# Chunked attention of the last block: keys and values held in rings of six blocks, queries in three buffers, bias in two

## The chip, the core and the metric

The kernel runs on one core of one Trainium2 chip. The metric is the device time of one execution in microseconds (us). A core has five engines with queues of their own: TensorE (PE, matrix products; its weight loads are shown apart as PEld), VectorE (DVE), ScalarE (ACT), GpSimd (POOL) and SyncE (SP), which here issues nearly all DMAs. Each engine works through its own instructions in order and waits on semaphores for the others. TensorE's clock has two levels, 2.4 and 1.2 GHz; the profile gives the granted share of the higher one.

## The reference

Two transformer blocks follow each other on 2048 tokens of width 1024. The change lies in the second one, in its chunked attention with a relative bias, for 8 heads of 64 values:

```
def chunked_relpos_attention(q, k, v, rel_bias):      # CHUNK = 64, N_LEFT_CHUNKS = 8, BAND = 576
    ...
    def one_chunk(c):
        start = c * CHUNK
        qc = lax.dynamic_slice_in_dim(q, start, CHUNK, axis=1)
        kc = lax.dynamic_slice_in_dim(k_pad, start, BAND, axis=1)
        vc = lax.dynamic_slice_in_dim(v_pad, start, BAND, axis=1)
        s = jnp.einsum('bqhd,bkhd->bhqk', qc, kc).astype(jnp.float32) * scale + bias[None]
        ...
        p = jax.nn.softmax(s, axis=-1).astype(v.dtype)
        return jnp.einsum('bhqk,bkhd->bqhd', p, vc)
```

So 64 queries attend to their own 64 keys and the 512 before them. The result is multiplied by silu of a gate. The same block has a second branch with sparse attention (256 chosen keys per query), gates for both branches and an output projection.

## The kernel before

The class `S3` computes the second block. Its projections write what they make into DRAM tensors: `QA` and `KA` (queries and keys of the chunked attention, transposed, each as a rounded part and the rest), `VA` (values, both parts), `QB` and `IQ` for the sparse branch, `SG` and `TZ` for gates. The attention loads from these.

The second block goes in stages (`run`, line 2784). After a first stage of normalization and projections there is `chunked(0)`, chunked attention for the first 1024 tokens; `sparse(range(10))`, sparse attention for ten blocks of 128 queries; `chunked(1)`, chunked attention for the other 1024 tokens; and a tail with the remaining sparse blocks and the output. Beside the first two runs a chain of work called `fill`: the projections of the first 1024 tokens that are still missing (`proj(0, range(8, 32))`), the load of the activations of the next tokens (`xn_load`, tiles `xnh` and `xnl`), and a part of the projections of those. What is left of `fill` runs alone before the next stage. Beside `chunked(1)` runs the rest of the projections, after `keep` has stored three tiles.

The order of instructions is made by the kernel's own planner. Every piece of work is a generator, a lane; `B.run` (line 306) asks the lanes in a fixed order, spawned pieces first, then the front lanes, then `back` (the fill), and begins again at the first as soon as one has issued something. A lane issues an instruction when `B.on` (line 245) says that by the planner's clock (`Clock.op`) its engine and its operands are ready. That clock holds a price for each instruction; for a DMA it is

```
        if eng == "sync":
            self.t[eng] = t + 0.05
            d = self.t["dma"] = max(self.t["dma"], t + 1.1) + cost
            end = d + 0.95
```

with cost = bytes / 3.6e5 us. The order so made is fixed in the program; on the chip the semaphores decide when each instruction starts.

Chunked attention goes by pairs of heads p = 0 to 3, and in each pair by units of 256 queries, c = 4·half to 4·half + 3. `a_loads` (line 2174) loads for each unit: at the first unit of a pair the bias `rb` (one buffer), then `K` of up to 768 keys (two DMAs, one per part, each on 64 partitions), `Q` (four DMAs), and `V` (one DMA); K, V and Q have two buffers each. With c = 0 there are 256 keys, with c = 1 there are 512, else 768. `a_unit` (line 2205) handles 128 queries (t = 0 or 1): score matmuls for both heads and both parts of Q, in pieces of at most 320 columns, under the lock `la`; DVE adds the bias and takes the maximum; ACT makes the exponentials, GpSimd scales them by the reciprocal sum. Then, under the lock `lb`, groups of two tiles are transposed (`pT`), split into two parts by ACT and DVE (`pp`) and multiplied with V (`a_pv`, line 2321). At the end of t = 1 the buffers of K, V and Q are free. ACT and DVE add up the parts (`up`), GpSimd finishes (`ot`), the gate is loaded (`gate_load`, line 2333; for the pair's gate `SG` must have been written by a projection of `fill`), GpSimd multiplies by it and SP stores to `YT`. Four units of 128 queries may be under way at a time (`pipe(self.a_units(half), 4)`, line 2883 on).

Of the kernel before, what the change touches and what calls it, by code (L numbers as in the profile page):

```python
# [22 lines left out]
T = 2048  # L23
# [11 lines left out]
class Clock:  # L35
# [45 lines left out]
    def at(self, a):  # L81
        n = a.tensor.name
        return max(self.ready.get(n, 0.0), self.free.get(n, 0.0))


def is_ap(x):
# [1754 lines left out]
BIG = -(2.0 ** 100)  # L1841
NSTEP = 12
SPLIT = 10


class S3:


    def __init__(self, b, X2, out, comb=None, skip=()):
        self.comb = comb  # L1850
        self.b, self.nc, self.I, self.X2, self.out = b, b.nc, b.I, X2, out
        nc = b.nc
# [276 lines left out]
    def ev_t(self, j, c, ps):  # L2129
        b, nc = self.b, self.nc  # L2130
        s = slice(c * 512, c * 512 + 512)
        if j < 8:
            p, isq = divmod(j, 2)
            sc = 0.125 if isq else 1.0
            hi, lo = yield from self.stage([128, 512], F32R, n=2)
            yield from b.on("scalar", ps, hi)
            nc.scalar.activation(hi, ps, AF.Copy, scale=sc)
            yield 1
            yield from b.on("vector", hi, lo)
            if isq:  # L2140
# [4 lines left out]
            dst = self.QA if isq else self.KA  # L2145
            yield 1
            yield from self.store(dst[0, p, :, s], hi)
            yield from self.store(dst[1, p, :, s], lo, None, ("qa" if isq else "ka", p, c))
        elif j < 16:
            i = (j - 4) % 8  # L2150
            t = yield from self.stage([128, 512])
            yield from b.on("scalar", ps, t)
            nc.scalar.activation(t, ps, AF.Tanh, scale=0.5)
            yield 1
            yield from b.on("vector", t)
            nc.vector.scalar_tensor_tensor(t, t, 1.0, ps, op0=OP.add, op1=OP.mult)
            b.done(ps)
            yield 1
            yield from self.store(self.SG[i, :, s], t, None, ("sg", i, c))
        else:  # L2160
# [10 lines left out]
            yield BLOCK  # L2171


    def a_loads(self, half):

        b, nc, P = self.b, self.nc, self.P
        for p in range(4):
            for c in range(4 * half, 4 * half + 4):
                yield from self.wait(("ka", p, c // 2), ("qa", p, c // 2), *[("va", c * 2 + i, p // 2) for i in range(2)])
                if c % 4 == 0:  # L2180
                    rb = yield from P.get([128, 2, 640], F32, "rb", bufs=self.nrb)
                    yield from b.on("sync", rb)
                    nc.sync.dma_start(rb, self.I["relb"][2 * p:2 * p + 2].rearrange("h q k -> q h k"))
                    yield 1
# [4 lines left out]
                k0 = c * 256 - 512  # L2189
                o = max(0, -k0)  # L2190
                for x in range(2):
                    r = slice(64 * x, 64 * x + 64)
                    nc.sync.dma_start(K[r, :, o:].bitcast(F32), self.KA[x, p, :, k0 + o:k0 + 768].rearrange("(e d) n -> d e n", e=2))
                    for y in range(2):
                        nc.sync.dma_start(Q[r, :, y].bitcast(F32), self.QA[y, p, :, c * 256:c * 256 + 256].rearrange("(e d) n -> d e n", e=2))
                yield 1
                nc.sync.dma_start(V[:, o // 128:].bitcast(F32), self.VA[k0 + o:k0 + 768, p * 256:p * 256 + 256].rearrange("(b t) n -> t b n", t=128))
                if c % 4 == 0:
                    yield from b.on("gpsimd", rb)
                    nc.gpsimd.memset(rb[0:64, :, 576:640], NEG)  # L2200
                    nc.gpsimd.memset(rb[64:128, :, 0:64], NEG)
                self.kv[p, c] = (Q, K, V, rb)
                yield 1

    def a_unit(self, p, c, t):
        b, nc, P = self.b, self.nc, self.P
# [1 line left out]
        while (p, c) not in self.kv:  # L2208
            yield BLOCK
        yield from self.la.get()  # L2210
        Q, K, V, rb = self.kv[p, c]
        k0 = max(0, 512 - blk * 128)
        kts = range(k0 // 128, 5)
        q_ = slice(t * 128, t * 128 + 128)
        sc = []
        st = b.small([128, 8], "ast", bufs=8)
        edges = [k0, 320, 640] if k0 < 320 else [k0, 640]
        for e in range(2):
            s = yield from P.get([128, 640], F32, "sc", bufs=4 if self.stored else 5)
            sc.append(s)  # L2220
            cur, turn = None, [0]
            for x in range(len(edges) - 1):
                w0, w1 = edges[x], edges[x + 1]
                ps = yield from b.bank("pS")
                kk = slice(t * 128 + w0, t * 128 + w1)
                yield from b.on("tensor", Q, K, ps)
                nc.tensor.matmul(ps[:, :w1 - w0], Q[:, e, 0, q_], K[:, e, kk], start=True, stop=False)
                nc.tensor.matmul(ps[:, :w1 - w0], Q[:, e, 1, q_], K[:, e, kk], start=False, stop=True)
# [14 lines left out]
        for g0 in range(0, len(groups), 2):  # L2243
# [8 lines left out]
            yield 1  # L2252
            pend.append((gs, pp, w))
            if len(pend) > 1:
                yield from self.a_pv(po4, V, t, *pend.pop(0), kts, po)
        b.done(*sc)
        while pend:
            yield from self.a_pv(po4, V, t, *pend.pop(0), kts, po)
        self.lb.free()
        if t == 1:  # L2260
            b.done(K, V, Q)
# [56 lines left out]
        w[0] = 1  # L2318
        yield 1

    def a_pv(self, po4, V, t, gs, pp, w, kts, po):
        b, nc = self.b, self.nc
        while not w[0]:
            yield BLOCK
        yield from b.on("tensor", pp, po, V)
        for i, (kt, e) in enumerate(gs):

            nc.tensor.matmul(po4[:, e].rearrange("p x q -> p (x q)"), V[:, t + kt, e * 128:e * 128 + 128], pp[:, i].rearrange("p x q -> p (x q)"),
                             start=kt == kts[0] and e == 0, stop=kt == kts[-1] and e == 1)
        b.done(pp)  # L2330
        yield 1
# [551 lines left out]
    def chunked(self, half, fill, sel):  # L2883

        with self.b.pool("s_a") as P:
            self.P, self.nrb, self.nsel, self.nrl, self.npp = P, 1, 1, 1 if sel else 2, 2 if half and sel else 3
            self.NM = (max(sel, default=0) + 1) * 128
            self.stored.update(sel)
            self.la, self.lb = Lock(1), Lock(1)
            self.kv = {}  # L2890
# [147 lines left out]
```

## Time and profile before

| | |
|---|---|
| median of three runs | 4234.5 us (4229.81 to 4241.1) |
| the profiled execution | 4238.96 us |
| its span, first to last instruction | 4237.1 us |
| mean granted TensorE clock | 0.939 |
| busy: DVE, ACT, POOL | 2733.3, 2263.5, 787.0 us |
| moved by DMA | 815.32 MB, 192 GB/s |
| HBM read, written | 589.56 MB, 229.65 MB |

The profile shows one execution. Rows of instructions name the tile that is written, then those that are read (`pS<-K,Q`); an engine's waits are put down to what ended them. Nearly all instructions have line 111 of the kernel, the helper that records them, so one goes by tiles. Of a window, the row shows each engine's busy time and number of instructions, then the mean granted clock, the mean busy share of the 16 DMA engines, and the rate. Busy times of TensorE are modelled at their ends.

### The profile page before, as it was taken

To read this page: it belongs to the slowest core of one execution; us is meant where nothing else is said; L and a number is where in the kernel's file an instruction comes from. 1 tells how busy PE (TensorE), PEld (TensorE's weight loads), DVE (VectorE), ACT (ScalarE), POOL (GpSimd) and SP (SyncE) were. 2 spreads that over 40 slices of the span, in tenths; PEclk is the share of its full clock that TensorE was granted. 3 is DMA by queue.
4 is the path that set the end of the run, shared out by engine and by line. 5 is a ranking of instruction groups with operands and counts; after the bars stand their busy time and mean duration, and the time that the engine had idled before them with its cause. 6 is when DMAs were issued, how large, how long until landed. Compare 5 with 4: busy or idle time off the path is not lost. (4 is left out here: it accounts for less than half of the span.)

```text
span 4237.1 us, 64813 instructions
## 1 busy us (share of the span) xinstructions
PE 3719.6 (88%) x21649; PEld 3211.7 (76%) x21649; DVE 2733.3 (65%) x7027; ACT 2263.5 (53%) x4628; POOL 787.0 (19%) x1474
## 2 busy tenths in 40 slices
PE   3999999979889995779888899998788979998895
PEld 2888788768768884778777798886677868997685
DVE  7866875787777776562445256777544248878772
ACT  3644645556456664342334167886444238876851
POOL 1310000131011112650334242000222101111000
PEclk9999999979999997899989989999899999999898
DMA  6232542144288886588888834432666488886154
GB/s 221 80 130 73 183 141 90 34 144 140 105 303 316 310 312 248 196 314 275 272 240 265 293 111 133 142 111 63 177 176 189 135 270 299 298 282 222 48 183 172
DMA packets 451953, 815.32 MB, mean 192 GB/s; under 512 B 129712, under 2 KB 269968, under 8 KB 450704
## 3 DMA queue, kind: packets, MB, share of 16 engines
q1 hardware_dynamic: 440080, 777.42, 55.2%
q0 software_dynamic: 11520, 33.57, 2.5%
q8 instruction: 176, 2.88, 0.3%
q14 instruction: 177, 1.45, 0.1%
HBM read 589.56 MB, written 229.65 MB: 193 GB/s over the span
## 5 line engine op out<-in xcount | busy, mean ns | idle before, releaser
L111 PE MATMUL pA<-xnl,whi 128*128 128x512 f32 x1024 | 417.8, 408 | 2.9 <-POOL whi L111 2.9
L111 DVE TENSOR_TENSOR wlo<-ld,whi 128x1024 fp32r<-128x1024 f32 x271 | 325.1, 1230 | 140.4 <-POOL whi L111 74.0
L111 ACT ACTIVATE pp<-pT 128x256 fp32r<-128x256 f32 (+1 forms) x568 | 260.8, 478 | 283.7 <-PE pT L111 277.4
L111 PE MATMUL pA<-xnh,wlo 128*128 128x512 f32 x1024 | 407.1, 398 | 2.3 <-DVE wlo L111 2.3
L111 PE MATMUL pA<-xnh,whi 128*128 128x512 f32 x1024 | 407.5, 398 | 0.0
L111 DVE TENSOR_TENSOR pp<-pT,pp 128x256 fp32r<-128x256 f32 (+1 forms) x568 | 295.9, 539 | 138.7 <-ACT pp L111 135.6
L111 PE MATMUL pA<-hlo,whi 128*128 128x512 f32 x832 | 352.8, 424 | 10.0 <-issue 6.6
L111 PE MATMUL pA<-hhi,wlo 128*128 128x512 f32 x832 | 329.7, 396 | 0.0
L111 PE MATMUL pA<-hhi,whi 128*128 128x512 f32 x832 | 328.9, 395 | 0.0
L111 PE MATMUL pU<-pp,vbS 128*128 128x256 f32 x1088 | 217.2, 311 | 34.5 <-DVE pp L111 23.3
L111 ACT ACTIVATE whi<-ld 128x1024 fp32r<-128x1024 f32 x212 | 213.3, 1052 | 50.7 <-PE pA L111 35.0
L111 DVE SCALAR_TENSOR_TENSOR acc<-rl,iw,acc 128x512 f32<-128x512 f32 (+3 forms) x304 | 212.7, 700 | 36.2 <-ACT rl L111 26.4
L111 PEld LDWEIGHTS pA<-xnh,wlo 128*128 128x128 f32 x1024 | 196.3, 192 | 47.3 <-DVE wlo L111 3.4
L111 PE MATMUL pA<-wlo,xnh 128*128 128x256 f32 (+1 forms) x672 | 205.0, 305 | 24.4 <-ACT st L111 5.9
L111 ACT ACTIVATE bias<-acc,sst 128x384 f32<-128x384 f32 (+13 forms) x168 | 219.9, 1309 | 8.6 <-DVE sst L111 6.1
L111 PEld LDWEIGHTS pA<-xnl,whi 128*128 128x128 f32 x1024 | 197.3, 193 | 33.6 <-POOL whi L111 3.3
L111 PEld LDWEIGHTS pA<-xnh,whi 128*128 128x128 f32 x1024 | 197.3, 193 | 30.2
L111 PEld LDWEIGHTS pU<-pp,vbS 128*128 128x128 f32 x1088 | 164.0, 198 | 53.6 <-DVE pp L111 33.5
L111 PE MATMUL pA<-whi,xnl 128*128 128x256 f32 (+1 forms) x672 | 200.0, 298 | 4.1 <-DMA xnl<-XND 4.1
L111 PE MATMUL pA<-whi,xnh 128*128 128x256 f32 (+1 forms) x672 | 199.8, 297 | 0.0
L111 PE MATMUL pS<-kbS,qd 128*128 128x512 f32 (+3 forms) x640 | 186.4, 391 | 13.5 <-DVE bst L111 9.6
L111 PE MATMUL pS<-K,Q 128*128 128x320 f32 (+3 forms) x480 | 117.7, 354 | 79.8 <-DMA Q<-QA 75.7
(491 smaller groups left out, 10993.7 us busy)
## 6 DMA issues: line engine op xcount, KB each, us to landing
whi<-W2P SPq DMA_DIRECT2D x172, 512.0 KB
wlo<-W2P SPq DMA_DIRECT2D x172, 512.0 KB
ld<-in_w_gu_dram SPq DMA_DIRECT2D x128, 512.0 KB
ld<-in_w_dn_dram SPq DMA_DIRECT2D x64, 512.0 KB
W2P<-whi SPq DMA_DIRECT2D x57, 512.0 KB
W2P<-wlo SPq DMA_DIRECT2D x57, 512.0 KB
Y<-ym SPq DMA_DIRECT2D x48, 512.0 KB
K<-KA SPq DMA_DIRECT2D x48, 384.0 KB
```

Of the source, the lines that this page charges most:

```text
L111: r = real(*a, **k)
```

## The change

Keys and values get one ring each, `K` and `V`, with places for KR = 6 blocks of 256 keys, for a whole stage. A lane of its own, `k_lane`, loads each block once per pair of heads and stage (two DMAs for K, one for V) as soon as the place is free; `pass_blocks` says after each unit which blocks no later unit of the pair needs. `Mark` is a stand-in by which the planner's clock knows when a block has landed; these DMAs are issued past the planner's recording and entered as one operation. `a_loads` loads only Q, with three buffers and two DMAs, from a `QA` whose layout is changed so that both parts of Q lie together. The bias has a lane of its own, `rb_lane`, and two buffers. In `a_unit` the score pieces are cut where the ring ends (`cut`), else at 320 as before. In `go` the lanes stand in the order units, `k_lane`, `a_loads`, `rb_lane`.

```
+KR = 6
-        self.QA = dr("QA", (2, 4, 128, T))
+        self.QA = dr("QA", (4, 4, 64, T))
...
+            dst = [self.QA[p, 2 * y:2 * y + 2, :, s].rearrange("e d n -> (e d) n") if isq else self.KA[y, p, :, s] for y in range(2)]
...
+    def rb_lane(self, half):
+        b, nc, P = self.b, self.nc, self.P
+        for p in range(4):
+            rb = yield from P.get([128, 2, 640], F32, "rb", bufs=self.nrb)
+            yield from b.on("sync", rb)
+            nc.sync.dma_start(rb, self.I["relb"][2 * p:2 * p + 2].rearrange("h q k -> q h k"))
...
+    def k_lane(self, half):
+        b, nc, P, c = self.b, self.nc, self.P, self.b.clock
+        self.K = P.tile([128, 2, 256 * KR], F32R, name="K", bufs=1)
+        self.V = P.tile([128, 2 * KR, 256], F32R, name="V", bufs=1)
+        n = 0
+        for p in range(4):
+            for j in range(max(0, 4 * half - 2), 4 * half + 4):
+                yield from self.wait(("ka", p, j // 2), *[("va", j * 2 + i, p // 2) for i in range(2)])
+                while n - KR >= self.passed:
+                    yield BLOCK
+                m = Mark(f"kv{half}_{n}")
+                c.free[m.tensor.name] = self.freed.get(n - KR, 0.0)
+                yield from b.on("sync", m)
+                o, s = n % KR, slice(j * 256, j * 256 + 256)
+                raw = nc._nc.sync
+                for x in range(2):
+                    raw.dma_start(self.K[64 * x:64 * x + 64, :, o * 256:o * 256 + 256].bitcast(F32),
+                                  self.KA[x, p, :, s].rearrange("(e d) n -> d e n", e=2))
+                raw.dma_start(self.V[:, 2 * o:2 * o + 2].bitcast(F32), self.VA[s, p * 256:p * 256 + 256].rearrange("(b t) n -> t b n", t=128))
+                c.op("sync", [m], [], 2 * 128 * 256 * 4 * 2 / 3.6e5)
...
     def a_loads(self, half):
...
-                K = yield from P.get([128, 2, 768], F32R, "K", bufs=2)
-                V = yield from P.get([128, 6, 256], F32R, "V", bufs=2)
-                Q = yield from P.get([128, 2, 2, 256], F32R, "Q", bufs=2)
-                yield from b.on("sync", K, V, Q)
...
+                Q = yield from P.get([128, 2, 2, 256], F32R, "Q", bufs=3)
+                yield from b.on("sync", Q)
                 for x in range(2):
...
+                    nc.sync.dma_start(Q[64 * x:64 * x + 64].rearrange("d y e n -> d (y e) n").bitcast(F32),
+                                      self.QA[p, :, :, c * 256:c * 256 + 256].rearrange("a d n -> d a n"))
                 yield 1
...
+                js = range(max(0, c - 2), c + 1)
+                while p not in self.rb or any((p, j) not in self.at_ring for j in js):
+                    yield BLOCK
...
+    def pass_blocks(self, p, c, half):
+        last = c if c == 4 * half + 3 else c - 2
+        t = max(self.b.clock.last.get(x.tensor.name, 0.0) for x in (self.K, self.V))
+        for j in range(max(0, 4 * half - 2), last + 1):
+            n = self.last_of[p, j]
+            if n >= self.passed:
+                self.freed[n] = t
+                self.passed = n + 1
...
-        edges = [k0, 320, 640] if k0 < 320 else [k0, 640]
+        cut = k0 + end - r0 if r0 + 640 - k0 > end else 320
+        edges = [k0, cut, 640] if k0 < cut else [k0, 640]
...
-            self.P, self.nrb, self.nsel, self.nrl, self.npp = P, 1, 1, 1 if sel else 2, 2 if half and sel else 3
+            self.P, self.nrb, self.nsel, self.nrl, self.npp = P, 1 if sel else 2, 1, 1 if sel else 2, 2 if half and sel else 3
...
-            self.go(pipe(self.a_units(half), 4), self.a_loads(half), self.sel_lane(sel), back=(fill,))
+            self.go(pipe(self.a_units(half), 4), self.k_lane(half), self.a_loads(half), self.rb_lane(half), self.sel_lane(sel), back=(fill,))
```

In both calls of `chunked`, `sel` is empty.

## Rows read from the trace of the kernel before

**Rows 1.** The page, busy us of each engine (share of the span) and its instructions.
```profile
PE 3719.6 (88%) x21649; PEld 3211.7 (76%) x21649; DVE 2733.3 (65%) x7027; ACT 2263.5 (53%) x4628; POOL 787.0 (19%) x1474
```

**Rows 2.** Windows: stretch and length, busy us (instructions), granted clock, DMA share, GB/s.
```profile
core 0: us, PE busy (x) PEld busy (x) DVE busy (x) ACT busy (x) POOL busy (x), PEclk, DMA share, GB/s
2003.00:2353.00 350.00, 310.24 (x1574) 260.85 (x1573) 177.13 (x549) 127.62 (x315) 136.58 (x195) 0.94 0.86 259
2353.00:2410.00 57.00, 57.00 (x255) 47.23 (x255) 9.26 (x8) 8.19 (x12) 9.42 (x14) 1.00 0.79 276
2410.00:2470.00 60.00, 46.74 (x250) 44.45 (x248) 13.13 (x48) 12.76 (x51) 18.98 (x100) 0.63 0.58 215
2470.00:2890.00 420.00, 406.58 (x2611) 361.25 (x2612) 298.06 (x847) 340.60 (x830) 72.63 (x253) 1.00 0.42 128
2890.00:3003.00 113.00, 79.68 (x434) 60.99 (x432) 72.94 (x213) 61.96 (x114) 6.51 (x19) 0.85 0.22 64
3003.00:3335.00 332.00, 291.52 (x1543) 251.98 (x1543) 162.41 (x571) 142.90 (x343) 94.25 (x163) 0.91 0.66 181
```

**Rows 3.** Waits of PE, 2003 to 2353: total us, times, longest.
```profile
PE pS L111 <- DMA Q<-QA: 26.6, 17, 5.6
PE pU L111 <- DVE pp L111: 4.8, 2, 3.0
...
PE pS L111 <- DMA K<-KA: 1.4, 1, 1.4
```

**Rows 4.** Waits of PE, 3003 to 3335.
```profile
PE pS L111 <- DMA Q<-QA: 36.7, 19, 5.7
PE pS L111 <- DMA K<-KA: 1.6, 1, 1.6
PE pT L111 <- POOL sc L111: 1.4, 2, 1.1
```

**Rows 5.** Timeline: start, duration, engine, operation [idle before it and what ended it].
```profile
2237.32 0.58 SPq L111 DMA_DIRECT2D K<-KA  x1
...
2237.95 1.25 SPq L111 DMA_DIRECT2D Q<-QA  x2
...
2239.24 0.60 SPq L111 DMA_DIRECT2D K<-KA  x1
...
2239.89 1.26 SPq L111 DMA_DIRECT2D Q<-QA  x2
...
2241.24 0.54 SPq L111 DMA_DIRECT2D V<-VA  x1
...
2247.57 1.70 PE L111 MATMUL pS<-K,Q 128*128 128x320 f32 x4 [4.03 <-DMA Q<-QA]
```

**Rows 6.** DMA issues of the whole kernel: count, KB each.
```profile
K<-KA SPq DMA_DIRECT2D x48, 384.0 KB
V<-VA SPq DMA_DIRECT2D x24, 768.0 KB
...
Q<-QA SPq DMA_DIRECT2D x128, 128.0 KB
...
rb<-in_relb_dram SPq DMA_DIRECT2D x8, 640.0 KB
```

**Rows 7.** Waits of PE, 2410 to 2470.
```profile
PE pA L111 <- DMA xnh<-XND: 5.6, 1, 5.6
PE pA L111 <- DMA xnl<-XND: 4.1, 1, 4.1
```

**Rows 8.** Waits of PE, 2890 to 3003.
```profile
PE pS L111 <- DMA Q<-QA: 12.3, 1, 12.3
```

**Rows 9.** Waits of SP's queue, 3003 to 3335.
```profile
SPq L111 <- POOL ot L111: 99.8, 22, 10.7
```

**Rows 10.** Waits of POOL, 3003 to 3335.
```profile
POOL ot L111 <- DMA sg<-SG: 82.5, 16, 9.7
```

**Rows 11.** Waits of POOL, 2003 to 2353.
```profile
POOL ot L111 <- DMA sg<-SG: 29.9, 9, 7.1
```

**Rows 12.** Timeline of SP, 2069 to 2072: the stage's first gate load.
```profile
2070.36 0.80 SPq L111 DMA_DIRECT2D sg<-SG  x2
```

More of the change, by code (lines that the diff above doesn't have):

```diff
@@ L83, in at, with __init__ @@
         return max(self.ready.get(n, 0.0), self.free.get(n, 0.0))
+class Mark:
+    class Named:
+        def __init__(self, name):
+            self.name = name
+    def __init__(self, name):
+        self.tensor = Mark.Named(name)
 def is_ap(x):
@@ L2171, in wait @@
             yield BLOCK
+    def rb_lane(self, half):
[4 more added lines that the diff above has]
+            nc.sync.dma_start(rb, self.I["relb"][2 * p:2 * p + 2].rearrange("h q k -> q h k"))
+            yield 1
+            yield from b.on("gpsimd", rb)
+            nc.gpsimd.memset(rb[0:64, :, 576:640], NEG)
+            nc.gpsimd.memset(rb[64:128, :, 0:64], NEG)
+            self.rb[p] = rb
+            yield 1
+    def k_lane(self, half):
[18 more added lines that the diff above has]
+                c.op("sync", [m], [], 2 * 128 * 256 * 4 * 2 / 3.6e5)
+                self.at_ring[p, j] = (o, m)
+                self.last_of[p, j] = n
+                n += 1
+                yield 1
     def a_loads(self, half):
@@ L2178, in a_loads @@
             for c in range(4 * half, 4 * half + 4):
[L2179 to L2184, printed above, removed]
-                K = yield from P.get([128, 2, 768], F32R, "K", bufs=2)
@@ L2186, in a_loads @@
-                V = yield from P.get([128, 6, 256], F32R, "V", bufs=2)
-                Q = yield from P.get([128, 2, 2, 256], F32R, "Q", bufs=2)
-                yield from b.on("sync", K, V, Q)
-                k0 = c * 256 - 512
-                o = max(0, -k0)
+                yield from self.wait(("qa", p, c // 2))
+                Q = yield from P.get([128, 2, 2, 256], F32R, "Q", bufs=3)
+                yield from b.on("sync", Q)
                 for x in range(2):
[L2192 to L2195, printed above, removed]
+                    nc.sync.dma_start(Q[64 * x:64 * x + 64].rearrange("d y e n -> d (y e) n").bitcast(F32),
+                                      self.QA[p, :, :, c * 256:c * 256 + 256].rearrange("a d n -> d a n"))
@@ L2210, in a_unit @@
         yield from self.la.get()
-        Q, K, V, rb = self.kv[p, c]
+        Q, ring, rb = self.kv[p, c]
+        K, V, marks = self.K, self.V, [m for _, m in ring.values()]
         k0 = max(0, 512 - blk * 128)
         kts = range(k0 // 128, 5)
+        place = lambda kt: ring[(blk - 4 + kt) // 2][0] * 2 + (blk + kt) % 2
+        r0, end = place(kts[0]) * 128, 256 * KR
         q_ = slice(t * 128, t * 128 + 128)
@@ L2224, in a_unit @@
                 ps = yield from b.bank("pS")
[L2225 to L2228, printed above, removed]
+                kk = (r0 + w0 - k0) % end
+                kk = slice(kk, kk + w1 - w0)
+                yield from b.on("tensor", Q, ps, *marks)
+                nc.tensor.matmul(ps[:, :w1 - w0], Q[:, 0, e, q_], K[:, e, kk], start=True, stop=False)
+                nc.tensor.matmul(ps[:, :w1 - w0], Q[:, 1, e, q_], K[:, e, kk], start=False, stop=True)
                 new = st[:, 2 * x + e:2 * x + e + 1]
@@ L2254, in a_unit @@
             if len(pend) > 1:
-                yield from self.a_pv(po4, V, t, *pend.pop(0), kts, po)
+                yield from self.a_pv(po4, V, place, *pend.pop(0), kts, po)
         b.done(*sc)
         while pend:
-            yield from self.a_pv(po4, V, t, *pend.pop(0), kts, po)
+            yield from self.a_pv(po4, V, place, *pend.pop(0), kts, po)
         self.lb.free()
         if t == 1:
-            b.done(K, V, Q)
+            b.done(Q)
+            self.pass_blocks(p, c, c // 4)
         up = yield from P.get([128, 2, 2, 128], F32, "up", bufs=1)
@@ L2319, in split_p, with a_pv @@
         yield 1
-    def a_pv(self, po4, V, t, gs, pp, w, kts, po):
+    def a_pv(self, po4, V, place, gs, pp, w, kts, po):
         b, nc = self.b, self.nc
@@ L2324, in a_pv @@
             yield BLOCK
-        yield from b.on("tensor", pp, po, V)
+        yield from b.on("tensor", pp, po)
         for i, (kt, e) in enumerate(gs):
-            nc.tensor.matmul(po4[:, e].rearrange("p x q -> p (x q)"), V[:, t + kt, e * 128:e * 128 + 128], pp[:, i].rearrange("p x q -> p (x q)"),
+            nc.tensor.matmul(po4[:, e].rearrange("p x q -> p (x q)"), V[:, place(kt), e * 128:e * 128 + 128], pp[:, i].rearrange("p x q -> p (x q)"),
                              start=kt == kts[0] and e == 0, stop=kt == kts[-1] and e == 1)
```

14 lines of the change are left out of this document (4 added, 10 removed).

## The prediction

> **What bounds the kernel now.** I first read the head of the page: TensorE is busy 88% of the span, far above any other engine [rows 1]. Then I cut the part that the change touches into six stretches [rows 2]. The two chunked-attention stages are 2003 to 2353 us and about 2987 to 3335 us; what lies between belongs to sparse attention, and after 3335 the rest of the projections runs alone. In the first stage TensorE has 350 − 310.2 = 39.8 us idle, in the second (from 3003) 332 − 291.5 = 40.5 us. The granted clock is 0.94 and 0.91 there, a mixture of its two levels, 2.4 and 1.2 GHz, so another 0.06 × 350 = 21 us and 0.09 × 332 = 30 us are lost at the low level. Where projections run alone, 2353 to 2410, the engine is full and the clock 1.00: these stages are bound by TensorE's work plus what it loses.
>
> Next I asked what TensorE waited for. In the first stage 26.6 us are waits of score matmuls for the load of Q and 1.4 us for that of K, 28.0 of 39.8 us; nothing else is above 5 us [rows 3]. In the second it is 36.7 + 1.6 = 38.3 of 40.5 us [rows 4]. Why the loads are late is seen in one look at the queue [rows 5]: the seven DMAs of one unit of 256 queries are issued from 2237.3 to 2241.8, 0.5 to 0.6 us each, and the first score matmul that needs them stands 4.0 us for them, until 2247.6. They cannot go earlier: K, V and Q have two buffers each, and one comes free only when the attention two units back is done. The order of instructions is fixed by the kernel's own clock, which charges 0.05 us per issue and 360 GB/s; in that stretch the chip needs ten times as long to issue, and the stage moves 259 GB/s at a DMA share of 0.86 [rows 2], about 300 at full share.
>
> **The change, part by part.**
>
> *Rings for K and V.* Now a unit loads up to three blocks of 256 keys: per pair of heads 1 + 2 + 3 + 3 = 9 blocks in the first stage and 12 in the second, 84 over four pairs by the loops of the code (most loads are of three blocks, [rows 6]). Afterwards each block is loaded once: 4 and 6 per pair, 40 in all. A block is 256 KB of K and 256 KB of V, so 44 × 0.524 = 23.1 MB go. At 274 GB/s per full share (181 at 0.66 in the second stage, [rows 2]) that is 84 us of the DMA engines, half per stage. It lowers their load and is not time by itself.
>
> *Issues on the queue.* K goes from 64 DMAs to 80, V from 32 to 40, Q from 128 to 64: 224 become 184. At 0.58 us that frees 23 us of SP in 680; SP is not the bound, so I count nothing.
>
> *Prefetch.* This is where the gain is. A third Q buffer lets Q go a whole unit earlier, and a new unit needs one new block for which one of six places is normally free. A unit takes about 21 us (332 us for 16), and the wait just seen is 4 us for loads that began 10 us before: one unit of lead covers it several times.
> First stage: 28.0 us of waits, and of the clock's 21 us the same share, 28.0/39.8, or 15 us: 43 us at stake. The transfers there stay dense (0.86, falling to some 0.75 without 42 us of them), and the attention will run closer together, which raises it again. I take 26; the ends are 0 and 43.
> Second stage: 38.3 us of waits and 38.3/40.5 of 30 us, 28 us: 66 at stake. The share is only 0.66. I take two thirds, 44; ends 15 and 66.
>
> *The ring's own wait.* A block's load must wait on SP until TensorE has read the old block in its place; behind it stand the weight loads, the stores of projections and the gate loads. K, V and Q have such a wait now for their buffers, and the place falls free earlier. Nothing, with ±10 us as bounds, the size of the longest waits of SP [rows 9].
>
> *Two bias buffers.* The 640 KB bias of the next pair [rows 6] no longer waits for the last scores of the pair before. It comes three times per stage and its lateness is already in the waits above: nothing more.
>
> *Score pieces.* The cut of the keys moves to the ring's end, which only the second pair of the first stage meets, in four units of 32. Pieces of 512 and 128 columns take the place of 320 and 320: as many matmuls and columns. Nothing. The new layout of QA stores the same bytes in as many DMAs: nothing.
>
> *A rule against it.* Where projections run alone, with their larger transfers, a full DMA share moves 276/0.79 = 349 GB/s; in the second attention stage, with its narrower loads, 274 [rows 2]. The Trainium skill (DMA: Bandwidth & Descriptors, Rules for kernel authors) asks for 128 partitions and at least 1 MiB per DMA, and the change cuts K's loads from 384 KB on 64 partitions to 128 KB. If they then moved at half the rate, 10.5 MB of K would cost 38 us more engine time, half of what is saved; the first stage's 26 us would fall to some 14 and the result be 12 us later. The two rates agree with the rule in sign but do not separate size from contention.
>
> *The start of the second stage.* Here there is no cover: TensorE stands 12.3 us for the first Q [rows 8], at the low clock. In the new order the lane of blocks comes before that of Q, and six places are free: 18 DMAs, some 10 us at 0.55 us, go ahead of the first Q. The first score waits about 8 us longer: −8, ends 0 and −16. In the first stage the same burst stands beside projections that fill TensorE.
>
> *What moves.* When loads are no longer waited for, the fixed order puts fewer projections into the attention stages; they run later, and their TensorE time is the same wherever they stand. Two later stretches lack work now. From 2410 to 2470, where the next tokens' activations are loaded, 13.3 us are idle and 0.37 × 60 = 22 us of clock are lost [rows 2]; TensorE waits for xnh and xnl there [rows 7]. From 2890 to 3003 the projections have run out: 33.3 us idle and 0.15 × 113 = 17 us of clock, of which 12.3 + 8 belong to the start just counted. Together 65 us that displaced projections could fill. But the last sparse blocks need some of those projections first, so they cannot be spread freely: I take a third, 22; ends −10 and 65.
>
> *Sum.* 26 + 44 + 22 − 8 = 84 us. The profiled execution took 4239.0 us (its span and 1.9 us around it): 4155. The median of the three runs is 4.5 us lower, so I predict **4150 us**. The optimistic ends give 4239 − 43 − 66 − 65 − 4.5 = 4060.
>
> **The rivals.**
>
> *The gate loads become the wait (slower).* Each of 64 units multiplies its output by a gate that SP loads late, and GpSimd, in order, stands for it: 82.5 us in the second stage [rows 10], 29.9 in the first [rows 11], 112 us in all or 1.75 us per unit. Behind it on GpSimd wait the softmax scalings that the transposes need, and SP waits for GpSimd 99.8 us in the second stage before storing [rows 9]. Against it: TensorE now waits for those scalings 1.4 us at most [rows 4]. That is because the loads of Q set the pace; with the attention closer together the slack goes. If all 112 us came onto TensorE, with 0.6 us of clock per us of idle (51 us of clock beside 80 of idle above), it would cost 180 against the 84 gained: 4150 + 180 = 4330. It decides from 84/1.6 = 53 us, 0.8 us per unit. Chance 0.10.
>
> *The change does not do what it says.* The ring is one tile. If its accesses were ordered as a whole, each block's load would wait for every score matmul issued before it, and the lead would shrink to that of now, about a unit. The bytes would go, the waits stay: 4234 less a few us, within 0.3%. Against it: the writes and reads name separate columns. Chance 0.08. (0.3%, 13 us, is about what a measurement of this kernel can tell from no change.)
>
> *The displaced projections fill everything.* All 65 us and most of both stages' losses are won: about 4060. For it: TensorE is full where projections stand alone [rows 2]. Against it: the gate of a pair is itself made by these projections; the first gate load of the stage comes only at 2070 us [rows 12], 67 us in, so the attention cannot run ahead at will. Chance 0.10.
>
> **How the numbers follow.** The forecast, a gain between 13 and 150 us, has 0.72. Faster by over 0.3%: 0.72 + 0.10 = 0.82; within 0.3%: 0.08; slower: 0.10. The range leaves out the slow rival and half of the fast one: 4070 to 4225, the upper end being a gain of 10 us, with the first stage unchanged and the second's at its low end.
>
> **What would show it.** Right: about 792 MB of transfers instead of 815.3; 40 loads of V and 64 of Q in the list of issues; TensorE's waits for Q and K below 10 us per stage; the attention stages shorter than 350 us each, the projections after them longer; the clock in both above 0.95. The second stage's first score would come about 20 us after its first load instead of 10. Wrong: the waits for Q and K gone and as much idle time put down to GpSimd's scalings or to DVE's pp instead; or loads of Q just as late, behind blocks that wait for TensorE; or a stretch without projections that is longer than 113 us.

## The result and the profile after

The changed kernel takes 4130.73 us (median of four runs, 4126.41 to 4133.16). The kernel before, run beside it, takes 4237.67 (four runs, 4229.81 to 4241.1). The ratio is 0.9749, with a 95% interval of 0.9731 to 0.9767: faster by 2.5%, 107 us. Forecast were 4150 us and a range of 4070 to 4225.

The head of the page of the changed kernel, its bytes, and the three loads in its list of DMA issues (count, KB each):

```profile
PE 3675.2 (89%) x21649; PEld 3189.6 (77%) x21649; DVE 2738.2 (66%) x7027; ACT 2265.0 (55%) x4628; POOL 788.6 (19%) x1474
...
DMA packets 442096, 792.24 MB, mean 192 GB/s; under 512 B 129072, under 2 KB 267280, under 8 KB 440848
```
```profile
Q<-QA SPq DMA_DIRECT2D x64, 256.0 KB
...
K<-KA SPq DMA_DIRECT2D x80, 128.0 KB
V<-VA SPq DMA_DIRECT2D x40, 256.0 KB
```

TensorE executes the same 21649 matmuls as in [rows 1], and 23.1 MB are gone, as forecast. To see where the 107 us come from, I cut both traces at the same events: the first load of each attention stage, the end of its last unit, the start of the tail. First the kernel before, by windows (columns as in [rows 2]); its first stage stands in [rows 2]:

```profile
2353.00:2988.00 635.00, 584.54 (x3532) 510.37 (x3531) 389.94 (x1100) 421.67 (x1001) 107.15 (x382) 0.95 0.42 134
2988.00:3335.00 347.00, 296.99 (x1556) 255.54 (x1557) 165.86 (x583) 144.74 (x347) 94.65 (x165) 0.89 0.68 186
3335.00:3419.00 84.00, 69.61 (x307) 57.15 (x306) 3.66 (x3) 11.75 (x16) 1.37 (x3) 0.93 0.43 144
3419.00:4237.00 818.00, 707.66 (x5038) 649.31 (x5038) 587.76 (x1448) 509.84 (x890) 95.75 (x146) 0.94 0.65 223
```

The same five stretches of the changed kernel, and behind them four shorter ones: the load of the next tokens' activations, the end of the stretch without projections, the second stage's start, and the rest of that stage:

```profile
2003.00:2315.00 312.00, 291.19 (x1554) 248.48 (x1553) 178.19 (x550) 128.09 (x316) 132.77 (x194) 0.97 0.81 256
2315.00:2938.00 623.00, 583.50 (x3559) 513.07 (x3557) 395.45 (x1101) 424.08 (x1002) 115.94 (x383) 0.95 0.43 138
2938.00:3230.00 292.00, 267.07 (x1530) 233.68 (x1531) 165.59 (x583) 143.98 (x345) 94.04 (x165) 0.94 0.60 174
3230.00:3319.00 89.00, 75.53 (x334) 62.02 (x332) 3.66 (x3) 12.74 (x17) 1.36 (x3) 0.94 0.42 144
3319.00:4131.00 812.00, 706.10 (x5038) 653.21 (x5038) 587.36 (x1448) 509.54 (x890) 94.79 (x146) 0.93 0.66 226
...
2400.00:2460.00 60.00, 47.39 (x249) 44.28 (x249) 19.16 (x71) 29.69 (x95) 18.16 (x92) 0.66 0.56 203
...
2873.00:2938.00 65.00, 52.88 (x285) 42.24 (x283) 40.04 (x109) 29.14 (x50) 3.96 (x11) 0.87 0.15 43
2938.00:2960.00 22.00, 2.36 (x7) 1.79 (x8) 1.24 (x6) 0.09 (x1) 0.40 (x2) 0.54 0.90 253
2960.00:3230.00 270.00, 264.71 (x1524) 231.89 (x1525) 164.36 (x578) 143.89 (x345) 93.64 (x163) 0.97 0.57 168
```

Read the lengths first: 350 to 312, 635 to 623, 347 to 292, 84 to 89, 818 to 812, that is −38, −12, −55, +5 and −6: −106. Then read why. In the first stage TensorE's idle time falls from 39.8 to 312 − 291.2 = 20.8 us, and what the low clock costs from 21 to 0.03 × 312 = 9 us: 31 of the 38. In the second stage idle goes from 50 to 25 us and clock from 0.11 × 347 = 38 to 17.5: 46 of the 55. The rest, 7 and 9 us, is some twenty matmuls per stage that now run later and a little less time in others. The tail, 5038 matmuls in either trace, took between 812 and 833 us over the traces of this study, so that −6 there says nothing.

What TensorE waits for, in the first stage and then in the second:

```profile
PE pT L122 <- POOL sc L122: 9.5, 6, 4.8
PE pU L122 <- DVE pp L122: 5.6, 4, 4.0
PE pS L122 <- DMA Q<-QA: 4.7, 2, 3.8
...
PE pS L122 <- DMA Q<-QA: 20.9, 1, 20.9
PE pS L122 <- DMA K<-KA: 2.5, 3, 1.9
PE pT L122 <- POOL sc L122: 1.9, 2, 1.7
```

Against [rows 3] and [rows 4], the waits for Q and K fall from 28.0 to 4.7 us and from 38.3 to 2.5, apart from one of 20.9 us at the second stage's start, which was 12.3 in [rows 8]. Of new waits there are 9.5 us for GpSimd's scalings. The timeline of that start (start, duration) shows the 18 DMAs of the six blocks ahead of the first Q:

```profile
2938.25 1.24 SPq L2218 DMA_DIRECT2D K<-KA  x2
2939.54 0.59 SPq L2220 DMA_DIRECT2D V<-VA  x1
...
2949.82 1.24 SPq L122 DMA_DIRECT2D Q<-QA  x2
...
2956.80 1.40 PE L122 MATMUL pS<-K,Q 128*128 128x320 f32 x4 [20.94 <-DMA Q<-QA]
```

### The profile page after: what moved, and what is told of

It reads as the page before. It is cut to its first block, busy times and chain, and to the rows that moved or that the text cites. A ratio compares the mean times of both kernels' runs of the same rounds, so it can differ in the third digit from the quotient of the medians.

```text
span 4131.0 us, 64766 instructions
## 1 busy us (share of the span) xinstructions
PE 3675.2 (89%) x21649; PEld 3189.6 (77%) x21649; DVE 2738.2 (66%) x7027; ACT 2265.0 (55%) x4628; POOL 788.6 (19%) x1474
## 4 chain that ended last, share of the span: by engine, by line
PE 35%; DMA 6%; DVE 5%; issue 4%; ACT 2%; SPq 1%; POOL 1%; DVEq 0%; POOLq 0%; ACTq 0%
PE pA L122 22%; PE pS L122 5%; PE pT L122 4%; PE pU L122 4%; DMA tz<-TZ 2%; DMA x<-IQ 1%; SPq L122 1%; DVE acc L122 1%; DVE pp L122 1%; DVE scb L122 1%; DMA x<-QB 0%; ACT bias L122 0%; ACT pp L122 0%; DMA V<-VA 0%; DMA Q<-QA 0%
## 5 line engine op out<-in xcount | busy, mean ns | idle before, releaser
L122 ACT ACTIVATE rl<-pS 128x512 f32<-128x512 f32 (+3 forms) x304 | 159.3, 542 | 58.0 <-PE pS L122 29.7
```

Source lines behind the costliest of these rows:

```text
L122: r = real(*a, **k)
```

## The experiments

Two theories were put against each other. **Lead** is the forecast's: the gain is that loads start earlier, since there are more buffers, and bytes and issues are worth nothing by themselves. **Bytes** says that it comes from loading less. All expectations were written before their run. Ratios are to the kernel before, run beside each.

### Parts of the change alone

*lead*: the kernel before, with a third buffer for each load; every byte is still loaded as often as before.

```
-                K = yield from P.get([128, 2, 768], F32R, "K", bufs=2)
-                V = yield from P.get([128, 6, 256], F32R, "V", bufs=2)
-                Q = yield from P.get([128, 2, 2, 256], F32R, "Q", bufs=2)
+                K = yield from P.get([128, 2, 768], F32R, "K", bufs=3)
+                V = yield from P.get([128, 6, 256], F32R, "V", bufs=3)
+                Q = yield from P.get([128, 2, 2, 256], F32R, "Q", bufs=3)
```

> The kernel before with 3 buffers each for K, V and Q, all else as it was: every unit still loads all its blocks (44 MB of K and V), one bias buffer. Lead: most of the gain without the rings, 4140 to 4170 us, waits for Q and K below 15 us per stage. Bytes: 4215 to 4240 us, waits as before (28 and 38 us).

Measured: 4173.5 us, 0.9833 [0.9810, 0.9855]: a gain of 65 us, near the first theory, but not all. The waits of TensorE for Q in its two stages (the second with its start):

```profile
PE pS L111 <- DMA Q<-QA: 14.8, 7, 3.7
...
PE pS L111 <- DMA Q<-QA: 24.2, 4, 12.7
```

Its two stages by windows:

```profile
2005.00:2368.00 363.00, 324.08 (x1658) 272.51 (x1657) 179.95 (x552) 131.30 (x319) 134.26 (x198) 0.96 0.89 266
...
2955.00:3292.00 337.00, 300.73 (x1628) 259.80 (x1629) 167.05 (x583) 147.03 (x349) 94.34 (x165) 0.92 0.74 199
```

26.6 became 14.8 us, and 12.3 + 36.7 became 24.2. So a lead of one more unit halves the waits and does not remove them. TensorE's idle time follows even less: 363 − 324.1 = 38.9 us in the first stage, against 39.8 before, because waits for `pp` (11.2 us) and for the scalings (6.3 us) take the place of those for Q; and 36.3 us in the second, against 50. The DMA share stays at 0.89 and 0.74. (The 65 us hold more than the buffers' worth; see the order of the projections, below.)

*q2*: the changed kernel with Q in two buffers.

```
-                Q = yield from P.get([128, 2, 2, 256], F32R, "Q", bufs=3)
+                Q = yield from P.get([128, 2, 2, 256], F32R, "Q", bufs=2)
```

> The changed kernel with Q in 2 buffers again; rings, the two loads of Q and the second bias buffer stay. Theory of the lead (loads come in time because they are issued a unit earlier; bytes are secondary): the 50 us or so of waits for Q come back, 4175 to 4210 us, and TensorE's waits for Q in the two attention stages are above 20 us each. Theory of the bytes (loads come in time because 23 MB fewer stand in the queue): no more than 15 us lost, 4130 to 4145 us.

Measured: 4149.6, 0.9780 [0.9760, 0.9801], a miss for both, between them. Without the third buffer, but with the rings, the stages wait for Q 6.9 and 4.4 us:

```profile
PE pS L122 <- DMA Q<-QA: 6.9, 7, 2.9
...
PE pS L122 <- DMA Q<-QA: 4.4, 4, 2.4
```

The second stage's start aside (22.6 us, put down to the bias there), the rings alone do to the waits what the third buffers alone do not. The 19 us to the changed kernel are at most the third buffer's worth beside rings: by the ratios they are 13, and the two intervals overlap.

*rb1*: the changed kernel with one bias buffer (`nrb` = 1).

> The changed kernel with one bias buffer. The prediction counted the second one at nothing: 4125 to 4140 us. The other view, that the bias at the turn of a pair is a wait of its own (three turns per stage, some 5 us each): 4145 to 4165 us.

Measured: 4138.4, 0.9752 [0.9725, 0.9779]. The ratio is that of the changed kernel; the second bias buffer is worth nothing that can be told.

### What bytes and issues cost

*twice*: the changed kernel, with each block of K and 7/8 of the V block loaded once more into tiles that nothing reads (811.92 MB, 120 more issues). The order of everything else stays.

```
+                k2, v2 = self.again[n % 2]
+                for x in range(2):
+                    raw.dma_start(k2[64 * x:64 * x + 64].bitcast(F32), self.KA[x, p, :, s].rearrange("(e d) n -> d e n", e=2))
+                raw.dma_start(v2.bitcast(F32), self.VA[s, p * 256:p * 256 + 224].rearrange("(b t) n -> t b n", t=128))
```

> The changed kernel in which every block of K and 7/8 of every block of V is loaded a second time into tiles that nothing reads: some 20 MB more, in the same order of all other instructions. Lead: at most 20 us lost, 4130 to 4150 us. Bytes: 4180 to 4230 us, with waits for Q or K of 20 us or more per stage.

Measured: 4209.5, 0.9919 [0.9896, 0.9941]. 79 us are lost of the 107 (72 by the ratios), although every ring, buffer and lead is there: the forecast's "not time by itself" falls. But bytes and issues grew together, so the next run adds the issues alone.

*issues*: as *twice*, but 16 columns or rows per DMA (793.57 MB); again nothing reads them.

```
+                s2 = slice(j * 256, j * 256 + 16)
+                for x in range(2):
+                    raw.dma_start(k2[64 * x:64 * x + 64, :, 0:16].bitcast(F32), self.KA[x, p, :, s2].rearrange("(e d) n -> d e n", e=2))
+                raw.dma_start(v2[:, :, 0:16].bitcast(F32), self.VA[s, p * 256:p * 256 + 16].rearrange("(b t) n -> t b n", t=128))
```

> The changed kernel, with three more DMAs per block as in the run twice, but each of 16 columns or rows, so that 120 issues are added and hardly any bytes; nothing reads what they bring. If the bytes were what cost 79 us in twice: 4130 to 4150 us, TensorE's waits in the two attention stages within 15 us of the changed kernel's. If it was the issues (120 of some 0.55 us on SP, ahead of the gate loads and Q): 4180 to 4215.

Measured: 4182.0, 0.9870 [0.9835, 0.9905]: 51 us lost (the interval makes it some 15 either way), at the low end of what was expected of issues. That is 51.2/120 = 0.43 us for each, most of the time that one takes on SP. The other 27.5 us of *twice* belong to 18.35 MB, 1.5 us per MB; by the ratios they are 21 us, some 18 either way, so the price of the bytes is known only roughly. TensorE's waits in the second stage, *issues* and then *twice*:

```profile
PE pS L122 <- DMA Q<-QA: 31.3, 1, 31.3
PE pT L122 <- POOL sc L122: 8.7, 6, 3.2
```
```profile
PE pS L122 <- DMA Q<-QA: 39.1, 2, 32.7
PE pT L122 <- POOL sc L122: 17.4, 5, 7.7
```

About 10 us of the loss in that stage is the first Q, behind 36 DMAs and not 18 (20.9 to 31.3 us). Of the other waits that the profile names there, those for the scalings grow most. In the first stage *issues* has one more wait, at the first score, that the changed kernel does not have:

```profile
PE pS L122 <- issue: 11.6, 1, 11.6
```

"issue" means that the profile shows nothing that was waited for. The first score comes 30 us after the stage's first load, 22 in the changed kernel, so the added DMAs ahead of the first Q are the likely cause; that is not shown. Some 22 of the 51 us are thus paid at the two starts; the other 29 us make 0.24 us per added issue.

*kact*: the changed kernel with the rings' 120 loads issued by ACT; no other engine's order changes.

```
-                raw = nc._nc.sync
+                raw = nc._nc.scalar
```

> The changed kernel with the 120 loads of the rings issued by ACT and not by SP; the order on every other engine stays as it is. If SP's time per issue is what the run issues showed (49 us for 120 more): SP gets some 66 us back, the second stage's first Q no longer stands behind 18 issues, its wait falls from 20.9 us to 8 to 14, and the time is 4090 to 4120. If ACT pays as much, by evictions that come later behind its own issues: TensorE's waits for ACT and DVE grow by 10 us or more, 4120 to 4145.

Measured: 4174.5, 0.9846 [0.9821, 0.9871]: 44 us slower than the changed kernel. Both expectations missed; ACT pays more than either said. The timeline of ACT at the second stage's start:

```profile
2957.54 1.26 ACTq L2218 DMA_DIRECT2D K<-KA  x2
...
2980.18 0.37 ACTq L2220 DMA_DIRECT2D V<-VA  x1
2980.60 0.83 ACT L122 ACTIVATE sc<-sc,ast 128x640 f32<-128x640 f32 x1 [22.89 <-DMA K<-KA]
```

The first exponential of the stage comes right behind the last of the 18 loads on its own queue. Most of the 22.9 us is still the time of the loads themselves: TensorE's first score starts at 2971.9, and by DVE's timeline the maximum that the exponential needs is done at 2975.5, so the queue holds it up by some 5 us. In both attention stages TensorE's waits for `pp` grow, from 5.6 to 11.1 and from 0.8 to 14.5 us. Together that is some 19 of the 44 us; where the rest arises was not followed.

### The rivals' mechanisms

*gate*: the changed kernel with a unit's gate loaded before its second half's matmuls, where it is stored by then.

```
+        g = None
+        if ("sg", p, blk // 4) in self.flags:
+            g = yield from self.gate_load(p, blk)
...
-        g = yield from self.gate_load(p, blk)
+        if g is None:
+            g = yield from self.gate_load(p, blk)
```

> The changed kernel with a unit's gate loaded ahead of its second half, where that gate is already stored, and not after its last matmul. If GpSimd's 57 us of waits for the gate (19.8 + 37.1) reach TensorE through the scalings, as the slow rival had it: TensorE's 9.5 + 1.9 us of waits for the scalings fall below 5, and the time to 4105 to 4123. If GpSimd has that time to spare: its waits for the gate fall below 25 us and the time stays at 4125 to 4137.

Measured: 4136.2, 0.9763 [0.9744, 0.9782], no gain. GpSimd's waits for the gate in the second stage, in the changed kernel and in *gate*:

```profile
POOL ot L122 <- DVE up L122: 40.0, 16, 5.5
POOL ot L122 <- DMA sg<-SG: 37.1, 14, 8.7
```
```profile
POOL ot L122 <- DVE up L122: 58.3, 16, 8.0
...
POOL ot L122 <- DMA sg<-SG: 2.6, 2, 1.8
```

GpSimd then waits for DVE in its place: it has the time to spare, and the gate loads bound nothing that shows in the time.

*first_q*: the changed kernel with the lanes of Q and bias ahead of that of the blocks.

```
-            self.go(pipe(self.a_units(half), 4), self.k_lane(half), self.a_loads(half), self.rb_lane(half), ...
+            self.go(pipe(self.a_units(half), 4), self.a_loads(half), self.rb_lane(half), self.k_lane(half), ...
```

> The changed kernel with the lanes of Q and of the bias ahead of that of the blocks. If the 18 DMAs of the six blocks ahead of the first Q make the second stage's first score wait: that wait falls from 20.9 us to 12 to 14, and the time to 4115 to 4128. If the first score stands for the blocks themselves, which then come after Q: the wait stays at 18 or more, 4126 to 4135.

Measured: 4145.3, 0.9788 [0.9750, 0.9825], not better, and above both ranges. The wait at the second stage's start does fall, from 20.9 us for Q to 13.6 for K, as the first theory said, but the time does not follow. With three later waits for K it is 19.5 us in all, where the changed kernel has 20.9 + 2.5 = 23.4; the stage takes 291 us against 292.

### The order of the projections

Comparing the traces showed something the forecast had not seen. In the kernel before, the loop of the first chunked stage went on writing out projections for 51 us after its last unit, until the first load of sparse attention at 2404.5 us; in the changed one these are 8.6 us, and in all runs above 5 to 10. `B.run` ends only when no lane and no spawned piece is left, and the fill kept spawning. Two runs end the loop at the last unit, one holds it open. (The edit of the first two stands in `go`, which every stage calls, so it also ends the other stages' loops early.)

*exit_before*, *exit_after*: the two kernels, with the fill no longer asked once the front lanes are done.

```
-            for g in first + self.spawned + lanes + back:
+            for g in first + self.spawned + lanes + (back if lanes or not drain else []):
...
-        self.b.run(*front, back=[g for g in back if g is not None])
+        self.b.run(*front, back=[g for g in back if g is not None], drain=True)
```

> The kernel before, with one edit: when the last unit of an attention stage is done, the loop that writes out the order ends at once, and the projections that it was filling up with go on in the next stage. Loads, buffers and bytes stay. If the 51 us between the first chunked stage's last unit and the first load of sparse attention are a loss of their own: that interval falls to 7 to 12 us, the stretch without projections before the second chunked stage (2890 to 3003) shrinks by 30 us or more, and the time is 4205 to 4225. If those projections only move: 4230 to 4245.

> The same edit on the changed kernel, whose interval there is already 8.6 us. If the interval is what counts: nothing is left to gain, 4120 to 4140. If the edit helps in some other way (at the ends of the other stages): below 4115, and the gain of exit_before says nothing on the interval.

Measured: *exit_before* 4189.4, 0.9882 [0.9845, 0.9919], twice the gain that was expected, 46 us (the interval makes it some 16 either way); *exit_after* 4124.7, 0.9733 [0.9698, 0.9768], the same as the changed kernel. The first three stretches of *exit_before*, cut as above:

```profile
2006.00:2359.00 353.00, 308.85 (x1575) 259.46 (x1575) 176.65 (x549) 127.98 (x316) 135.07 (x195) 0.95 0.86 257
2359.00:2965.00 606.00, 561.98 (x3530) 490.79 (x3528) 393.62 (x1100) 423.41 (x1001) 112.77 (x382) 0.99 0.45 141
2965.00:3294.00 329.00, 290.71 (x1585) 249.49 (x1586) 165.63 (x583) 144.52 (x348) 94.38 (x165) 0.94 0.72 200
```

Between the stages 635 us become 606, nearly all by the clock (0.95 to 0.99, 26 us); the second stage has 347 to 329. TensorE's idle time in the two attention stages is 44.2 and 38.3 us here, 82.5 in all.

*exit_after* gains nearly as much between the stages. Its second and third stretch, and the 60 us in which the activations are loaded:

```profile
2310.00:2912.00 602.00, 570.96 (x3559) 499.26 (x3558) 395.89 (x1101) 424.83 (x1002) 115.88 (x383) 0.99 0.45 143
2912.00:3216.00 304.00, 273.26 (x1558) 238.70 (x1559) 166.27 (x583) 144.99 (x347) 94.52 (x165) 0.94 0.59 171
...
2400.00:2460.00 60.00, 56.37 (x405) 51.07 (x404) 37.64 (x123) 40.52 (x135) 27.33 (x131) 0.97 0.71 248
```

623 us become 602, again with the clock at 0.99: while the activations are loaded TensorE is now busy for 56.4 of 60 us at 0.97, where the changed kernel has 47.4 at 0.66. But the second stage grows from 292 to 304 us, with 28 more matmuls in it, and the tail from 812 to 824, within its spread.

*hold*: the changed kernel, made to keep its loop open as the kernel before did.

```
+    def hold(self, us):
+        while self.passed < 16:
+            yield BLOCK
+        t = self.b.clock.now
+        while self.b.clock.now < t + us:
+            yield BLOCK
```

> The changed kernel, made to behave as the kernel before at the end of the first chunked stage: its loop is held open for 45 us of the kernel's own clock after the last unit, so that projections are written out there before sparse attention begins. Rings, buffers and bytes stay. If the late handover was worth the 46 us that exit_before gained: the interval is 40 to 55 us, the stretch without projections before the second stage is longer than 90 us, and the time 4160 to 4180. If the interval costs only beside late loads of Q: below 4145.

Measured: 4140.3, 0.9772 [0.9750, 0.9794]. The interval came, 47.7 us, and the time went up by 10, not by 46. The first two windows are that interval and the rest up to the second stage:

```profile
2315.00:2363.00 48.00, 48.00 (x213) 39.72 (x212) 9.51 (x8) 6.81 (x10) 9.37 (x14) 1.00 0.77 277
2363.00:2930.00 567.00, 535.76 (x3350) 475.65 (x3348) 383.91 (x1093) 416.07 (x992) 100.59 (x369) 0.95 0.41 129
```

48 + 567 = 615 us stand against 623 in the changed kernel: the projections only moved (what this trace has more is its tail, 828 against 812 us). The theory that the interval is a loss of its own falls for the changed kernel, which has lost the clock between its stages without it (0.95, and 0.96 over the 615 us of *hold*). With the loop's end made alike, the change is worth 4189.4 − 4124.7 = 65 us (both early) or 4237.7 − 4140.3 = 97 us (both late). Between the stages the early end removes 29 and 21 us in the two kernels; the difference lies mostly in the second stage, 18 us shorter in one and 12 longer in the other. Why stays open. It also bears on *lead*, whose loop ends early (9.9 us): against *exit_before*, third buffers are worth 4189.4 − 4173.5 = 16 us and not 65, with intervals that overlap. Of the 82.5 us of idle time in the two stages they leave 38.9 + 36.3 = 75.2; the changed kernel leaves 20.8 + 24.9 = 45.7.

### A version that beats both

*k_one*: *exit_after* with K stored as `(4, 2, 128, T)`, both parts of a head under each other, so that a block of K is one DMA on 128 partitions.

```
-                for x in range(2):
-                    raw.dma_start(self.K[64 * x:64 * x + 64, :, o * 256:o * 256 + 256].bitcast(F32),
-                                  self.KA[x, p, :, s].rearrange("(e d) n -> d e n", e=2))
+                raw.dma_start(self.K[:, :, o * 256:o * 256 + 256].bitcast(F32), self.KA[p, :, :, s].rearrange("e q n -> q e n"))
```

> The run exit_after (4124.7 us) with K laid out so that a block of K is one DMA of 128 partitions and 256 KB, not two of 64 partitions and 128 KB: 40 issues fewer in the two attention stages, and 32 more for the stores of K, which need two DMAs each and stand among the projections. By the price of the run issues, 51 us for 120 or 0.42 us each: 17 us less in the stages, of which the stores give back between nothing (projections do not stand for SP) and 14: 4107 to 4122. If only the issues at a stage's start count (6 of 18 ahead of the first Q): 4 us there, 4117 to 4124 in all. If the stores of K, which the blocks wait for, come later and hold the blocks up: above 4130.

Measured: 4110.3 us (five runs, 4105.29 to 4115.47), 0.9703 [0.9690, 0.9716], 14 us below *exit_after*, whose interval is wide, and faster than the changed kernel by intervals that do not meet. The timeline of its second start, and its two stages by windows:

```profile
2908.68 0.37 SPq L2229 DMA_DIRECT2D K<-KA  x1
2909.10 0.46 SPq L2230 DMA_DIRECT2D V<-VA  x1
2909.61 0.46 SPq L2229 DMA_DIRECT2D K<-KA  x1
...
2916.01 1.29 SPq L122 DMA_DIRECT2D Q<-QA  x2
```
```profile
2002.00:2304.00 302.00, 287.74 (x1547) 246.70 (x1546) 176.97 (x548) 127.28 (x315) 132.17 (x194) 0.98 0.80 262
...
2909.00:3205.00 296.00, 272.48 (x1557) 238.49 (x1558) 166.22 (x583) 144.82 (x346) 94.28 (x165) 0.95 0.58 176
```

A block takes SP 0.9 to 1.0 us where it took 1.9, the six blocks are out after 7.3 us and not 11.6, and the stages are 8 us shorter each than in *exit_after* (310 and 304). It changes the number of issues and the shape of the loads together; which of them counts was not tried apart.

## Why the prediction was right, and where its terms were off

**The wait was named rightly, what removes it was not.** TensorE stood for late loads of Q, with the clock behind them, and in the changed kernel these waits are nearly gone. But loads that start earlier, which were to bring most of the gain, did little alone (*lead*). 40 loads of V, 64 of Q and 792 MB are there; the stages are 312 and 292 us, below 350; the projections after the second are longer (84 to 89). Q and K make TensorE wait less than 10 us per stage but for the start. The clock is 0.97 in the first stage; in the second it is 0.94, not the 0.95 that was named, because of the start (0.54 there, 0.97 after it).

**The sum came out 22 us short**: 84 forecast, 106 in the traces.

| term | forecast | measured |
|---|---|---|
| first stage | 26 of 43 at stake | 38 |
| second stage, start included | 44 − 8 = 36 | 55 |
| what moves | 22 | 12 − 5 = 7 |
| tail | not counted | 6, within its spread |

*The two stages* were mis-sized by 12 and 19 us, and the step behind it is "it lowers their load and is not time by itself", with the issues that were counted at nothing because "SP is not the bound". The forecast put all of the gain on the earlier start of loads. The run *lead* has an earlier start and no fewer bytes; half of the waits stay, and nearly all of the idle time. At the prices of *issues* and *twice*, the 40 issues and 23.1 MB that are saved are worth 17 + 35 = 52 us. That is an extrapolation from loads added to loads removed; without the stages' starts, where the change saves no issues, it is 10 + 35. Between *lead* and the changed kernel lie 43 us (36 by the ratios). So of the 107 us some 35 to 50 come, by this estimate, from loading less, in fewer issues. One rival is left in that step: the blocks and Q now go each when its own buffer is free, where K, V and Q of a unit had to wait for all three, and no run tries this alone. *twice* keeps these lanes and loses most of the gain, but with 304 such DMAs, and the kernel before had 224. The rest of the 107 us is that of more buffers and of the order of the projections, 16 to 65 us and up to 46, which the runs do not part further.

That the time came so near the forecast is therefore partly luck: earlier loads, priced at 26 + 44 = 70 us, brought far less where they were tried alone, and fewer bytes and issues, priced at nothing, and an order of projections that nobody had looked at made up for it. The forecast's own sign for the issues was in its text: from 0.58 us each it worked out that 23 us of SP go free, and counted them at nothing. SP need not be the busiest engine for that. It goes through its DMAs in order, so each issue delays all that stands behind it, Q and gates among them.

*The start of the second stage* was right in size: −8 forecast, 12.3 to 20.9 us measured. It is the whole burst that is waited for and not Q alone: in *q2*, *rb1* and *gate* the same wait, 22.0 to 22.6 us, is put down to the bias, and *first_q*, with another order, has a shorter wait, for K, and no better time.

*What moves* was too large by 15 us. The two stretches that displaced projections were to fill are as empty as before: where the activations are loaded, 60 − 47.4 = 12.6 us idle at a clock of 0.66 (13.3 at 0.63 before); from the last projections to the first score, 12.1 + 19.6 = 31.7 us idle (33.3 before). Only some 20 matmuls per stage moved. What did move by the loop's end, some 42 us of projections, the forecast had not seen; *exit_after* shows that the first of the two stretches can be filled.

*The rule against the change.* The first stage moves 256/0.81 = 316 GB/s per full DMA share and the second 174/0.60 = 290, where it was 301 and 274. No slowing by the narrower loads of K shows, and the 12 us that the forecast worked out beside the rule did not come. *k_one* moves 327 and 303, its neighbour *exit_after* 319 and 290: 3 and 5% more with 256 KB on 128 partitions. That has the sign of the rule in the Trainium skill (DMA: Bandwidth & Descriptors, Rules for kernel authors), 128 partitions and at least 1 MiB per DMA, at a small price. The same table of the Trainium skill advises against two transfers to disjoint halves of the partitions; *k_one*, 14 us faster with one, agrees in sign, though its issues change along with the shape.

**The rivals.** The gate loads did not become the wait: GpSimd's waits for them fell from 112 to 57 us (19.8 + 37.1), and *gate* removes them without a gain. What spoke for this rival, scalings that come late, did appear, 9.5 and 1.9 us, and grew in *issues* and *twice*. That the ring is ordered as one tile is excluded by the waits that are gone. That displaced projections fill everything is excluded by the two stretches above; and yet *k_one*, at 4110 us, shows that 4130 is not the end.

## What to carry to other kernels

Price an issue by what its queue holds behind it, not by how busy the queue is: here one in-order queue carried all loads of stages that waited for loads; 40 fewer and wider DMAs went with a gain of 14 us, and moving 120 to the queue of an engine that the softmax needs lost 44. When a prefetch is to remove a wait, try it alone, with the bytes unchanged, and read the engine's idle time beside the named waits; here it left half of the waits and nine tenths of the idle time, because other waits took their place. And in a kernel whose order is planned, compare the order of the two programs first: more buffers can move a stretch of unrelated work, and an edit of that order alone gained 46 us here.

## What the hardware showed that was not expected

- The time of an issue on SP differed with its neighbours. The same load of V, 256 KB on 128 partitions, took 0.59 us behind loads of K on 64 partitions, and 0.46 behind loads of K on 128 in *k_one*; why is not shown. A K load took 0.62 us on 64 partitions and mostly 0.37 to 0.47 on 128, for twice the bytes. Two K loads of 16 columns took 1.22 us in *issues*, as long as two of 256 (1.23).
- On ACT's queue the same 18 issues took 23 us (2957.5 to 2980.6) where SP took 11.6 (2938.25 to 2949.8).
- The same issues took from 3 to 7 us: the four of Q behind the second start's first unit took SP 3.07 us in the changed kernel, 3.92 in *issues*, 3.85 in *k_one*, and 7.29 in *kact*, where ACT issued the rings at the same time. What stretches them is not shown.
